# Two-layer hybrid network in fp32 on one core: half-partition operations get their own durations in the plan, the parameters arrive as 16 rows, and dummy products stand in gaps at both ends

## The chip, the cores and the metric

The program runs on one core of one Trainium2 chip. The core has a matrix engine (TensorE, PE in the profile; its weight loads are shown as PEld), a vector engine (VectorE, DVE), an activation engine (ScalarE, ACT), GpSimd (POOL) and a queue engine (SyncE, SP) that here issues every DMA. The metric is the device time of one execution in microseconds; lower is better. Results of TensorE land in PSUM, which this kernel uses as eight banks of 128 partitions by 512 fp32 values.

## The reference

A network of two layers on 1024 tokens by 1024 features in fp32, cut here to what is computed:

```python
for layer in range(2):
    h = rmsnorm(x, mix_norm[layer])
    y = sliding_window_attention(h, ...) if layer == 0 else hgrn2_recurrence(h, ...)
    x = x + y
    h = rmsnorm(x, mlp_norm[layer])
    x = x + square(relu(h @ w_up[layer])) @ w_down[layer]     # 1024 -> 4096 -> 1024
return rmsnorm(x, final_norm)
```

The attention has 16 query heads over 4 key/value heads of 64 features, a window of 128 tokens, partial rotary embedding and one sink logit per head. The recurrence is a gated linear recurrence over chunks of 64 tokens with 8 heads of 128 features.

## The kernel before

The activations lie transposed: features on the 128 partitions, 512 tokens (one half of the sequence) along the free axis. A matrix product in fp32 is made of three products of split operands (`mm3`): each factor is split into a high part in fp32r (`wh` for weights, made by a CAST on ACT or DVE) and the remainder (`wl`, made by a subtraction on DVE), and high x high, high x low and low x high are summed in one PSUM bank. Bank tags are `p` (four banks) and `q` (four banks). `wr` are raw weights as loaded (six buffers), `wh` and `wl` have five buffers each, `a` and `t` are tiles of 128x512, `m` a smaller pool of them, `sm` are tiny ones, `c` constants, `d` tiles in DRAM. The large products use one or two levels of Strassen's scheme.

No engine's order is written by hand. The program records all operations with their operands (`Schedule.add`), each with a planned duration for each engine that could do it. `forward` then lays them out in time with a list scheduler, engine by engine, by rank; `backward` works out the latest start (`late`) of each operation; four passes alternate and the best one is issued (`order`, `issue`). So a planned duration decides which engine does an operation and where it stands in that engine's row, and the engine then runs its row strictly in that order. `act`, `copy`, `tt` and `stt` (lines 435 to 461) give the durations: for ACT reading PSUM 52 ns and 0.834 ns per column, for DVE 70 ns and 1.04 ns per column, whatever the number of partitions.

The stages, with their places in the profiled execution:

- Head (0 to about 8 us). `first_loads` issues the loads of x, the parameters `par` (norm gains and bounds, 64 columns on 128 partitions) and the first weights. `warm` has TensorE multiply a zero tile by itself eight times (16 rows in the trace, since a product of plain fp32 runs as two). `scaled` multiplies x by a gain out of `par`, ACT for the high part and DVE for the low part.
- `qkv(0)` for the first half of the tokens (to about 82 us): three column groups of 512 columns. Group 0 holds keys and values, groups 1 and 2 queries. In each group four `p` banks (one per block of 128 tokens) collect 8 x 3 products each, 96 in all. When a group is complete, DVE reads the four banks with `stt` (scale by the token's factor, add the bias; `projected`, `keys_values`), and only then can the next group write those banks. `keys_values` also turns the keys by TensorE into a `q` bank and takes them out with half-partition operations on 64 partitions: `copy` on ACT for the high part and `tt` on DVE for the low part, 64x128 each, line 1202 onward.
- Attention of both halves, interleaved with `qkv(1)`, then the output projection (to about 330 us). `attend` (line 1206) takes turned queries out of a bank by one `act` and one `stt` on 64x512 each.
- MLP of layer 0 (to about 900 us), HGRN layer (to about 1450 us; `recurrence` copies score blocks of 64 partitions by 256 columns on ACT, lines 1505 to 1507), MLP of layer 1 (to about 2065 us).
- The end. `final` normalises the output, called three times: for the first half of the tokens (about 2038 us), and for the second half in two pieces of 256 tokens (about 2052 and 2065 us). `sum_squares` adds squares, once over seven of the eight feature tiles (`first`) and once over the eighth (`last`); `token_rstd` takes their means by TensorE products with a 128x1 constant into a `q` bank, and computes 1/sqrt in five tiny operations; `spread` turns the token factors into a 128-partition bank by products with the identity `self.ident` (tile `c67`). DVE multiplies three quarters of the output tiles by that bank, and POOL, which cannot read it, one quarter with a copy `rs` that ACT makes of the bank. Each result goes out by a DMA from SP.

Of the kernel before, what the change touches and what calls it, by code (L numbers as in the profile page):

```python
# [17 lines left out]
P = 128  # L18
# [13 lines left out]
HD = 64  # L32
# [115 lines left out]
class Schedule:  # L148
# [8 lines left out]
    def add(self, ways, outs, ins, tail=0.0, form=None, table=None):  # L157
# [4 lines left out]
        if any(isinstance(v, View) and v.buf.tag == "p" for v in ins):  # L162
            lead = max(lead, EVACUATE)
        op.rank, op.after, op.first = (len(self.ops) - lead, len(self.ops)), [], []
# [23 lines left out]
    def forward(self):  # L188
# [41 lines left out]
        while True:  # L230
# [131 lines left out]
class Net:  # L362
# [72 lines left out]
    def act(self, out, in_, func, n=TH, bias=None, scale=1.0, accum=None):  # L435
        kw, cost = {}, (52 if in_.buf.tag in "pq" else 94) + n * 0.834
# [11 lines left out]
    def copy(self, out, in_, n=TH, engines=("ACT",), psum=True):  # L448
        ways = {"ACT": self.call(self.nc.scalar.copy, out, in_) + ((52 if psum else 94) + n * 0.834,)}
# [3 lines left out]
    def tt(self, e, out, x, y, alu, n=TH):  # L453
        cost = {"DVE": 70 + n * 1.04, "Pool": 147 + n * 2.105}
# [4 lines left out]
    def stt(self, out, x, scalar, y, op0, op1, n=TH):  # L459
        self.op("DVE", self.nc.vector.scalar_tensor_tensor, [out], [x, scalar, y], 70 + n * 1.04 + 60 * isinstance(scalar, View),  # L460
# [71 lines left out]
    def token_rstd(self, acc, inner=1.0, outer=1.0, n=TH, keep=False, more=()):  # L532
# [50 lines left out]
    def square_relu(self, m, hf, c, psum):  # L583
# [6 lines left out]
        else:  # L590
# [7 lines left out]
            self.s.add({"ACT": (on_act, 2 * (94 + TH * 0.834)), "DVE": (on_dve, 70 + TH * 1.04)}, [c], [c])  # L598
# [534 lines left out]
    def first_loads(self):  # L1133
# [3 lines left out]
        self.x = [[None] * NH for _ in range(KT)]  # L1137
        for kt in range(KT):
# [5 lines left out]
            if kt == 0:  # L1144
                self.dma(self.par, self.io["par"], 4 * P * N_PAR)
# [31 lines left out]
    def keys_values(self, n, ps, r):  # L1177
# [16 lines left out]
        for i, (first, end) in enumerate(K_SPANS):  # L1194
# [540 lines left out]
```

## Time and profile before

| | us |
|---|---|
| median of 3 runs (lowest, highest) | 2078.83 (2077.93, 2079.97) |
| the profiled execution, its own time | 2078.63 |
| its span, from the first to the last instruction | 2076.9 |
| TensorE busy, share of the span | 2058.8, 99% |
| VectorE busy, share of the span | 1894.4, 91% |
| ScalarE busy, share of the span | 1109.9, 53% |
| mean granted TensorE clock | 0.997 |

Nearly all instructions carry line 416 (`issue` records them all there), so the groups are told apart by tiles and shapes. A busy TensorE says little by itself, since the ends of its matmuls are modelled; the views by window and by time show where its rows stop following one another, and how far apart they stand.

### The profile page before, as it was taken

To read this page: it belongs to the slowest core of one execution; us is meant where nothing else is said; L and a number is where in the kernel's file an instruction comes from. 1 tells how busy PE (TensorE), PEld (TensorE's weight loads), DVE (VectorE), ACT (ScalarE), POOL (GpSimd) and SP (SyncE) were. 2 spreads that over 40 slices of the span, in tenths; PEclk is the share of its full clock that TensorE was granted. 3 is DMA by queue.
4 is the path that set the end of the run, shared out by engine and by line. 5 is a ranking of instruction groups with operands and counts; after the bars stand their busy time and mean duration, and the time that the engine had idled before them with its cause. 6 is when DMAs were issued, how large, how long until landed. Compare 5 with 4: busy or idle time off the path is not lost.

```text
span 2076.9 us, 35708 instructions
## 1 busy us (share of the span) xinstructions
PE 2058.8 (99%) x12220; PEld 1746.1 (84%) x12220; DVE 1894.4 (91%) x3929; ACT 1109.9 (53%) x2265; POOL 58.2 (3%) x121
## 2 busy tenths in 40 slices
PE   9999999999999999999999999999999999999998
PEld 7778878888898888888888888888888888888887
DVE  8899999999999989989998888888999999998995
ACT  6465867655565423556444444443766556532453
POOL 4030000000000000000000000000000000000000
PEclk9999999999999999999999999999999999999999
DMA  6212368877779967641322222677887768996822
GB/s 214 81 56 72 118 218 262 290 223 247 226 246 306 339 218 246 220 137 67 109 95 99 103 102 90 214 237 235 284 265 248 238 224 265 309 315 212 270 64 82
DMA packets 225846, 407.43 MB, mean 196 GB/s; under 512 B 25344, under 2 KB 30464, under 8 KB 225664
## 3 DMA queue, kind: packets, MB, share of 16 engines
q1 hardware_dynamic: 225664, 405.16, 58.9%
q8 instruction: 96, 1.57, 0.3%
q14 instruction: 86, 0.70, 0.1%
HBM read 321.17 MB, written 83.89 MB: 195 GB/s over the span
## 4 chain that ended last, share of the span: by engine, by line
PE 96%; DVE 2%; issue 1%; ACT 1%; DMA 0%; POOL 0%; POOLq 0%; SPq 0%; ACTq 0%; DVEq 0%
PE p L416 51%; PE q L416 44%; DVE a L416 1%; DVE t L416 1%; ACT a L416 1%; DVE wl L416 0%; ACT t L416 0%; DMA wr<-in_wqkv 0%; DVE m L416 0%; ACT wh L416 0%; POOL a L416 0%; POOLq L1709 0%; SPq L416 0%; ACT m L416 0%; DVE sm L416 0%
## 5 line engine op out<-in xcount | busy, mean ns | idle before, releaser
L416 PE MATMUL p<-a,wh 128*128 128x512 f32 (+1 forms) x2880 | 806.3, 364 | 0.0
L416 PE MATMUL q<-a,wh 128*128 128x512 f32 x2112 | 653.2, 391 | 0.0
L416 PEld LDWEIGHTS p<-a,wh 128*128 128x128 f32 x2880 | 515.2, 189 | 83.1 <-issue 0.4
L416 PE MATMUL p<-a,wl 128*128 128x512 f32 (+1 forms) x1440 | 522.2, 363 | 0.0
L416 PEld LDWEIGHTS q<-a,wh 128*128 128x128 f32 x2112 | 389.7, 188 | 75.3
L416 PE MATMUL q<-a,wl 128*128 128x512 f32 x1056 | 410.6, 389 | 0.0
L416 PEld LDWEIGHTS p<-a,wl 128*128 128x128 f32 x1440 | 271.9, 189 | 40.0
L416 ACT CAST wh<-wr 128x512 fp32r<-128x512 f32 x252 | 155.8, 620 | 186.3 <-PE p L416 117.5
L416 DVE TENSOR_TENSOR wl<-wr,wh 128x512 fp32r<-128x512 f32 x352 | 240.6, 688 | 6.3 <-ACT wh L416 2.5
L416 DVE TENSOR_TENSOR wl<-m,wh 128x512 fp32r<-128x512 f32 x338 | 231.6, 686 | 11.1 <-ACT wh L416 5.8
L416 ACT CAST wh<-m 128x512 fp32r<-128x512 f32 x252 | 155.8, 620 | 154.1 <-PE q L416 88.7
L416 PEld LDWEIGHTS q<-a,wl 128*128 128x128 f32 x1056 | 198.4, 188 | 42.0
L416 ACT ACTIVATE t<-t 128x512 f32<-128x512 f32 x244 | 153.8, 632 | 113.6 <-DVE t L416 107.8
L416 DVE TENSOR_TENSOR a<-t,a 128x512 fp32r<-128x512 f32 (+2 forms) x314 | 207.3, 678 | 6.6 <-PE q L416 5.5
L416 DVE TENSOR_TENSOR t<-t,t 128x512 f32<-128x512 f32 (+3 forms) x337 | 196.8, 599 | 5.7 <-ACT t L416 4.5
L416 ACT COPY t<-q 128x512 f32<-128x512 f32 (+2 forms) x201 | 111.4, 559 | 97.8 <-PE q L416 84.7
L416 ACT CAST a<-t 128x512 fp32r<-128x512 f32 (+1 forms) x199 | 119.2, 611 | 66.3 <-PE q L416 40.3
L416 PE MATMUL p<-wh,a 128*128 128x512 f32 x384 | 127.6, 403 | 5.1 <-DVE a L416 4.1
L416 DVE TENSOR_TENSOR m<-wr,wr 128x512 f32<-128x512 f32 (+1 forms) x188 | 121.4, 646 | 3.3 <-DMA wr<-in_down 1.5
L416 DVE TENSOR_TENSOR t<-t,p 128x256 f32<-128x256 f32 x294 | 118.6, 414 | 0.0
L416 PEld LDWEIGHTS q<-t,t 128*64 128x64 f32 (+1 forms) x2160 | 95.9, 144 | 12.9 <-issue 8.1
L416 PE MATMUL q<-t,t 128*64 128x32 f32 (+2 forms) x2160 | 104.8, 229 | 0.2 <-ACT t L416 0.2
(129 smaller groups left out, 2387.0 us busy)
## 6 DMA issues: line engine op xcount, KB each, us to landing
t<-d SPq DMA_DIRECT2D x548, 256.0 KB, 4.1
d<-t SPq DMA_DIRECT2D x244, 256.0 KB, 3.3
wr<-in_down SPq DMA_DIRECT2D x224, 256.0 KB, 4.1
wr<-in_up SPq DMA_DIRECT2D x178, 256.0 KB, 3.9
wr<-in_win SPq DMA_DIRECT2D x68, 256.0 KB, 2.8
a<-d SPq DMA_DIRECT2D x60, 256.0 KB, 3.9
wr<-in_wqkv SPq DMA_DIRECT2D x48, 256.0 KB, 2.9
d<-a SPq DMA_DIRECT2D x48, 256.0 KB, 3.8
```

Of the source, the lines that this page charges most:

```text
L416: fn(*[place(a) for a in args], **{k: place(v) for k, v in kw.items()})
```

## The change

It has three parts that the planner then turns into a new order of the whole program.

1. Plan. Operations on half of the partitions get 125 ns more on ACT and 105 ns more on DVE (`HALF`): the 64x128 copies and subtractions in `keys_values`, the 64x512 ones in `attend`, the 64x256 copies in `recurrence`. The two-step square of a rectified tile on ACT gets 150 ns more. A new rule in `forward` lets an engine stay idle for a more urgent operation that becomes ready soon (`WAIT`). In `keys_values` DVE's subtraction is recorded before POOL's clearing.
2. Head. The parameters come as 16 rows of 512 values in one load, issued first; four TensorE transposes turn them into a `p` bank and ACT copies the bank to `par`. `warm` does ten products.
3. End, in `token_rstd` and `final`, wherever `more` is given, that is in all three calls of `final`: all means of `first` come before those of `last`; four dummy products of the identity with itself follow those of `first` and five more follow those of `last`, each set into a `q` bank of its own. For the two pieces of 256 tokens `spread` is done twice, into two banks, one for DVE and one for ACT's copy; and one pair of output tiles is multiplied and stored in two pieces.

The diff, cut to its core:

```diff
+HALF = {"ACT": 125.0, "DVE": 105.0}
+WAIT = 0.5
-WARM = 8
+WARM = 10
+ROWS = 16
...
+            if p and e != "PE" and op.late is not None:
+                soon = p[0][2]
+                gap, lost = p[0][0] - t, t + op.ways[e][1] - p[0][0]
+                if not soon.engine and soon.late is not None and gap < WAIT * lost and soon.late < t + op.ways[e][1] \
+                        and op.late > soon.late and len(soon.ways) >= 1:
+                    heapq.heappush(r, (op.rank, op))
+                    free_at[e] = p[0][0]
+                    continue
...
-    def warm(self, zero):
-        ps = self.psum()
-        for _ in range(WARM):
+    def warm(self, zero, n=WARM, tag="p"):
+        ps = self.psum(tag)
+        for _ in range(n):
             self.mm(ps[:, :P], zero, zero, True, True, P, 4)
...
-        for j in range(nb):
-            parts = [acc, *more]
-            for i, z in enumerate(parts):
-                self.mm(ps[:, j : j + 1], z[:, j * P : j * P + P], self.mean, i == 0, i == len(parts) - 1, P, 2)
+        parts = [acc, *more]
+        for i, z in enumerate(parts):
+            for j in range(nb):
+                first, last = (j == 0, j == nb - 1) if more else (True, True)
+                self.mm(ps[:, j : j + 1], z[:, j * P : j * P + P], self.mean, i == 0 and first, i == len(parts) - 1 and last, P, 2,
+                        skip_group_check=bool(more))
+            if more and z is acc:
+                self.warm(self.ident, 4, "q")
+        if more:
+            self.warm(self.ident, 5, "q")
...
+        rows = self.t()
+        self.dma(rows[:ROWS], self.io["par"], 4 * P * N_PAR)
+        ps = self.psum()
+        n = N_PAR // ROWS
+        for k in range(n):
+            self.op("PE", self.nc.tensor.transpose, [ps], [rows, self.ident], 109, ps[:, k * ROWS : k * ROWS + ROWS],
+                    rows[:ROWS, k * P : k * P + P], self.ident[:ROWS, :ROWS], form="whole")
+        self.copy(self.par, ps[:, :N_PAR], N_PAR)
...
-            if kt == 0:
-                self.dma(self.par, self.io["par"], 4 * P * N_PAR)
...
-                self.copy(dst, src, P)
+                self.copy(dst, src, P, more=HALF["ACT"])
+                self.tt("DVE", kl[g][r, c].only(n), src, dst.bitcast(F32), ALU.subtract, P, HALF["DVE"])
                 self.ts("Pool", ks[g][o, c].only(n), dst, 1.0, None, ALU.mult, None, P)
-                self.tt("DVE", kl[g][r, c].only(n), src, dst.bitcast(F32), ALU.subtract, P)
...
-                    self.act(s[r], pq[r], AF.Copy, scale=HD**-0.5)
-                    self.stt(s[o], pq[r], HD**-0.5, s[r].bitcast(F32), ALU.mult, ALU.subtract)
+                    self.act(s[r], pq[r], AF.Copy, scale=HD**-0.5, more=HALF["ACT"])
+                    self.stt(s[o], pq[r], HD**-0.5, s[r].bitcast(F32), ALU.mult, ALU.subtract, more=HALF["DVE"])
...
-        r, rs = self.spread(self.token_rstd(first, n=n, more=[last]), n), self.t()[:, :n]
-        self.copy(rs, r, n)
+        y = self.token_rstd(first, n=n, more=[last])
+        r, rs = self.spread(y, n), self.t()[:, :n]
+        self.copy(rs, self.spread(y, n) if n < TH else r, n)
...
+            step = 1 if n < TH and k == per else per
+            for i in range(0, per, step):
+                c = slice(i, i + step)
+                part = pair[:, c].only(*range(k + i, k + i + step))
+                self.tt(e, part, part, share.unsqueeze(1).to_broadcast([P, step, n]), ALU.mult, step * n)
```

What moves is seen in three places. In the rows below a tile's name has its buffer number and then its number in the program, which differ between the two programs for the same thing.

DVE in `qkv(0)`, just ahead of the read-out of column group 1 (`a<-p,sm,a`, banks p125 and on before, p127 and on after); `a<-a,c,a` are low parts of the second half's x, `t<-t,t` sums of squares, `t<-q,a` the 64x128 subtractions. Before:

```order
L416 TENSOR_TENSOR t120_196<-q124_668,a116_701 64x128
L416 SCALAR_TENSOR_TENSOR a224_843<-a210_545,c01_65,a223_609 128x512 [waits DMAHW2_49]
L416 TENSOR_TENSOR t229_665<-t229_665,t236_836 128x512 [waits Activation_49]
L416 TENSOR_TENSOR wl177_854<-wr175_662,wh176_845 128x512 [waits DMAHW0_49,Activation_49]
L416 SCALAR_TENSOR_TENSOR a226_858<-a211_555,c01_65,a225_722 128x512 [waits DMAHW3_49]
L416 SCALAR_TENSOR_TENSOR a228_865<-a212_571,c01_65,a227_729 128x512 [waits DMAHW4_49]
L416 TENSOR_TENSOR a91_872<-a90_548 128x256
L416 SCALAR_TENSOR_TENSOR a153_876<-p125_565,sm50_451,a61_396 128x512 [waits PE_49]
L416 SCALAR_TENSOR_TENSOR a156_881<-p126_579,sm50_451,a61_396 128x512 [waits PE_49]
```

After:

```order
L428 TENSOR_TENSOR wl179_831<-wr177_709,wh178_824 128x512 [waits DMAHW0_49,Activation_49]
L428 TENSOR_TENSOR t104_362<-q114_639,a100_379 64x128
L428 TENSOR_TENSOR t119_174<-q114_639,a115_727 64x128
L428 TENSOR_TENSOR t120_187<-q114_639,a116_733 64x128
L428 TENSOR_TENSOR t121_192<-q114_639,a117_737 64x128
L428 TENSOR_TENSOR t122_198<-q114_639,a118_743 64x128
L428 SCALAR_TENSOR_TENSOR a220_853<-a209_424,c01_65,a219_494 128x512
L428 SCALAR_TENSOR_TENSOR a155_861<-p127_578,sm52_473,a63_558 128x512 [waits DMAHW3_49,PE_49]
L428 SCALAR_TENSOR_TENSOR a158_867<-p128_590,sm52_473,a63_558 128x512 [waits PE_49]
```

Counted from the read-out of group 0 to that of group 1, DVE's row holds 66 instructions before and 59 after: four 64x128 subtractions, two `a<-a,c,a` and one 128x256 difference now stand behind the read-out.

ACT in the same column group; `wh<-wr` are the high parts of weights, `a<-q 64x128` the half-partition copies, `t<-a` squares. Before:

```order
L416 CAST a114_694<-q124_668 64x128
L416 CAST a115_697<-q124_668 64x128
L416 CAST a116_701<-q124_668 64x128
L416 ACTIVATE t231_714<-a207_497 128x512 [waits DVE_49]
L416 ACTIVATE a225_722<-a211_555,c01_65 128x512 [waits DMAHW3_49]
L416 ACTIVATE a227_729<-a212_571,c01_65 128x512 [waits DMAHW4_49]
L416 ACTIVATE t232_737<-a208_510 128x512 [waits DVE_49]
L416 CAST wh148_745<-wr147_466 128x512 [waits PE_49]
L416 CAST wh151_751<-wr150_480 128x512 [waits DMAHW5_49,PE_49]
```

After:

```order
L428 CAST a118_743<-q114_639 64x128
L428 CAST a115_727<-q126_647 64x128 [waits PE_49]
L428 CAST a116_733<-q126_647 64x128
L428 CAST wh172_754<-wr171_569 128x512 [waits DMAHW4_49,Activation_49]
L428 CAST wh153_760<-wr152_547 128x512 [waits DMAHW2_49,PE_49,Activation_49]
L428 CAST a117_737<-q126_647 64x128
L428 CAST wh147_772<-wr146_528 128x512 [waits DVE_49,DMAHW0_49,PE_49,Activation_49]
L428 CAST a118_743<-q126_647 64x128
L428 CAST wh150_785<-wr149_536 128x512 [waits DMAHW1_49]
```

The eight squares, which stood between and behind the copies, now stand in a row ahead of all of them (rows 43 to 50 of ACT's row, behind `a229`), each in a buffer of its own, where seven of the eight shared one before; the high parts that group 1 still needs (`wh147`, `wh150`, `wh153`) stand behind the copies. Over the attention layer, 24 CASTs that DVE did before are now ACT's.

PE at the end, where the first piece of 256 tokens of the second half is finished (`p5026` and `p5028` are its last bank, `q5883` and `q5887` the bank of means, `p5023` and `p5025` banks of the last piece). Before:

```order
L416 MATMUL p5026_21383<-a5848_24269,a5845_24223 128x256
L416 MATMUL p5026_21383<-a5847_24217,a5846_24275 128x256
L416 MATMUL q5883_24485<-c23_69,t5875_23906 128x1 [waits DVE_49]
L416 MATMUL p5023_21353<-a5812_24036,a5810_24025 128x256
L416 MATMUL p5023_21353<-a5813_24041,a5810_24025 128x256
L416 MATMUL p5023_21353<-a5812_24036,a5811_24033 128x256
```

After:

```order
L428 MATMUL p5028_21380<-a5849_24213,a5848_24298 128x256
L428 MATMUL q5887_24497<-c23_69,t5879_23773 128x1 [waits DVE_49,PE_49]
L428 MATMUL q5887_24497<-c23_69,t5879_23773 128x1
L428 MATMUL q5888_24502<-c67_67 128x128 [waits PE_49]
L428 MATMUL q5888_24502<-c67_67 128x128 x3
L428 MATMUL q5889_24508<-c67_67 128x128 [waits PE_49]
L428 MATMUL q5889_24508<-c67_67 128x128 x2
L428 MATMUL q5887_24497<-c23_69,t5886_24510 128x1 [waits Activation_49]
L428 MATMUL q5887_24497<-c23_69,t5886_24510 128x1
L428 MATMUL q5889_24508<-c67_67 128x128 x2
L428 MATMUL p5025_21354<-a5814_24046,a5812_24035 128x256
```

Seven of the nine dummy products (`c67` alone on the right) stand between the two sets of means and two behind them; before, products of the last piece stood there. In the call for the first half of the tokens the nine dummies stand likewise between products, four behind the first four means and five behind the others.

More of the change, by code (lines that the diff above doesn't have):

```diff
@@ L446, in act, with copy, tt @@
                 out, in_, func, scale=scale, table=TABLES.get(func), **kw)
[L448 to L449 removed]
+    def copy(self, out, in_, n=TH, engines=("ACT",), psum=True, more=0.0):
+        ways = {"ACT": self.call(self.nc.scalar.copy, out, in_) + ((52 if psum else 94) + n * 0.834 + more,)}
         ways["DVE"] = self.call(self.nc.vector.tensor_copy, out, in_) + (70 + n * (1.04 if psum else 0.52),)
         self.s.add({e: ways[e] for e in engines}, [out], [in_])
[L453 to L454 removed]
+    def tt(self, e, out, x, y, alu, n=TH, more=0.0):
+        cost = {"DVE": 70 + n * 1.04 + more, "Pool": 147 + n * 2.105}
         engines = ("DVE",) if e == "any" else (e,)
```

22 lines of the change are left out of this document (11 added, 11 removed).

## The prediction

> **What bounds the kernel now.** I read the page first, then the chain of waits, then windows chosen along it, then the rows by time at the four places where TensorE's rows do not follow one another.
>
> ```profile
> span 2076.9 us, 35708 instructions
> PE 2058.8 (99%) x12220; PEld 1746.1 (84%) x12220; DVE 1894.4 (91%) x3929; ACT 1109.9 (53%) x2265; POOL 58.2 (3%) x121
> PE 96%; DVE 2%; issue 1%; ACT 1%; DMA 0%; POOL 0%; POOLq 0%; SPq 0%; ACTq 0%; DVEq 0%
> ```
>
> TensorE is busy 2058.8 of 2076.9 us and carries 96% of the chain. Whatever a new order of the other engines can give is thus among some 18 us of idle time, the places where its clock is halved, and the few microseconds ahead of its first and behind its last product; every row added to TensorE costs its length wherever TensorE has no gap. The windows (busy us of PE, PEld, DVE, ACT and POOL with instructions, granted clock, DMA share, GB/s) say where the gaps are:
>
> ```profile
> core 0: us, PE busy (x) PEld busy (x) DVE busy (x) ACT busy (x) POOL busy (x), PEclk, DMA share, GB/s
> 54.00:58.05 4.05, 0.15 (x2) 0.03 (x1) 4.02 (x8) 0.62 (x1) 0.00 (x0) 1.00 0.21 65
> 55.06:58.47 3.41, 0.42 (x2) 0.41 (x3) 3.38 (x6) 0.00 (x0) 0.00 (x0) 1.00 0.25 77
> 58.47:61.89 3.42, 3.42 (x10) 2.64 (x9) 3.42 (x11) 0.00 (x0) 0.00 (x0) 0.50 0.09 23
> 62.00:300.00 238.00, 235.69 (x1361) 189.15 (x1360) 216.03 (x497) 157.18 (x497) 23.20 (x50) 1.00 0.32 104
> 300.00:2038.00 1738.00, 1737.79 (x10388) 1482.47 (x10387) 1604.56 (x3235) 906.03 (x1669) 8.58 (x20) 1.00 0.64 211
> 2038.00:2065.20 27.20, 27.20 (x232) 27.16 (x230) 16.39 (x40) 6.99 (x18) 2.59 (x2) 1.00 0.31 117
> 2065.51:2068.93 3.42, 0.83 (x6) 0.78 (x7) 1.50 (x7) 1.02 (x3) 0.00 (x0) 1.00 0.00 0
> ```
>
> One stall of 3.9 us at 54 us, with DVE busy throughout; 3.4 us at half clock right behind it, which cost 1.7 us more; 2.3 us of small waits over the rest of the attention layer; 0.2 us in 1738 us after that; none from 2038 to 2065 us, where `final` is called for the first time and the second. The reader is to see that the whole middle has nothing to win.
>
> The sums are made against the profiled execution, 2078.63 us, and the result is set against the median of the runs, 2078.83 us, 0.2 us more. A measurement of this kernel can tell about 0.2%, 4.2 us, from no change.
>
> **Column group 1 of the first projection.** DVE's and ACT's rows there, and twelve TensorE products in a row:
>
> ```profile
> 29.88 0.47 DVE L416 SCALAR_TENSOR_TENSOR t<-p,sm,a 128x256 f32<-128x256 f32 x1
> ...
> 33.39 0.18 DVE L416 TENSOR_TENSOR t<-t,t 128x32 f32<-128x32 f32 x1
> ...
> 52.28 1.19 DVE L416 TENSOR_TENSOR t<-q,a 64x128 fp32r<-64x128 f32 x4
> ...
> 55.38 1.40 DVE L416 SCALAR_TENSOR_TENSOR a<-a,c,a 128x512 fp32r<-128x512 f32 x2
> 56.70 0.41 DVE L416 TENSOR_TENSOR a<-a 128x256 f32<-128x256 f32 x1
> 57.15 2.73 DVE L416 SCALAR_TENSOR_TENSOR a<-p,sm,a 128x512 f32<-128x512 f32 x4
> ```
>
> ```profile
> 38.95 2.82 ACT L416 CAST a<-q 64x128 fp32r<-64x128 f32 x10
> 41.80 0.63 ACT L416 ACTIVATE t<-a 128x512 f32<-128x512 f32 x1
> 44.08 1.13 ACT L416 CAST wh<-wr 128x512 fp32r<-128x512 f32 x2
> ```
>
> ```profile
> 378.49 2.75 PE q L416 x12
> ```
>
> The four banks of group 1 are full at 54.0, but DVE reads them from 57.15: it had work left in its row. The plan counted a 64x128 subtraction as 70 + 128 x 1.04 = 203 ns and a 64x128 copy as 52 + 128 x 0.834 = 159 ns; the rows show 1.19 / 4 = 298 and 2.82 / 10 = 282 ns. So twenty of each made DVE 1.9 us and ACT 2.5 us later than planned. The added 105 and 125 ns give 308 and 284 ns: the new durations are the measured ones.
>
> What the new order makes of it, worked out in two ways. By difference: between the two read-outs DVE has 4 x 0.30 + 2 x 0.70 + 0.41 = 3.0 us less, so it reads from 57.15 - 3.0 = 54.1 instead; one read of 0.68 us and the way to TensorE leave a stall of 1.0 us. By ACT's row: the squares no longer wait for each other's buffer, so they run from about 33.5, when the rotary operations at 33.39 free their buffers, for 0.63 + 7 x 0.52 = 4.3 us, with casts' spacing of 1.13 - 0.62 = 0.51 as the nearest row; 18 copies at 0.282 take 5.1, two casts 1.1, one copy and `wh147` 0.9 us: ready at 44.9. TensorE wants it after 60 products at 2.75 / 12 = 0.229 and eight transposes at about 0.1, 14.5 us after group 1 began (54.0 - 23.0 = 31.0): 45.5. Its low part on DVE follows at about 45.9, 0.2 late. I take 0.8, between 0.2 and 1.0. A wait this short leaves the clock alone, as no window above with most of its time busy is followed by 0.50. The term is 0.8 - 3.9 - 1.7 = **-4.8**, at best -5.6, at worst -2.0, if 1.9 us of waiting halve the clock again.
>
> **The rest of the attention layer.** The same correction applies to 64x512 operations, and 24 casts pass from DVE (216 of 238 us busy) to ACT (157), which has the room: 24 x 0.51 = 12 us. At most the 2.3 us go; as a row rearranged by the same rules can also miss, the bound above is one more stall like that at 54 us, +4. I take **-1.0**, less than half of what is there.
>
> **HGRN layer and both MLPs.** 0.2 us is to be won. All of it is rearranged, 45 more casts pass to ACT (906 of 1738 us busy), and the 64x256 copies are planned longer: **0**, bounds -0.2 and +3, a stall of the known kind without its half clock.
>
> **The head.**
>
> ```profile
> 1.05 3.78 PE L416 MATMUL p<-t 128*128 128x128 f32 x16 [1.05 <-DVE t L416]
> ...
> 4.99 0.71 ACT L416 ACTIVATE a<-a,c 128x512 fp32r<-128x512 f32 x1
> ...
> 5.75 0.79 PE L416 MATMUL p<-wh,a 128*128 128x512 f32 x1 [0.92 <-DVE c L416]
> ...
> 6.34 0.63 PE L416 MATMUL p<-wl,a 128*128 128x512 f32 x1
> ...
> 6.77 0.63 PE L416 MATMUL p<-wh,a 128*128 128x512 f32 x1
> ...
> 8.48 1.22 PE L416 MATMUL p<-wh,a 128*128 128x512 f32 x2 [0.23 <-DVE a L416]
> ...
> 10.74 0.40 PE L416 MATMUL p<-wl,a 128*128 128x512 f32 x1
> ```
>
> Sixteen rows of warming take 3.4 us to the last one's start, at half clock; twenty take 4.2, so the four new transposes start at 5.5 and end about 5.9. The loads are not the reason: `par` is now issued first, and the first weight tile of that place arrived at 3.8. ACT's copy of 64 columns (0.25, as for other 64-column operations, and the way from TensorE) lets `a<-a,c` start at 6.45, and the first product at 6.45 + 0.71 + 0.05 = 7.2, against 5.75. The stall before 8.48 falls away, as DVE now does that low part at 7.4 to 8.1, ahead of the second weight tile. Products stand 0.43 apart until 10.7 and 0.23 after. By 10.7 there are 10.2 products before and 8.2 after: 2 x 0.23 = **+0.5**. If the clock comes up before 7.2, it is 15 by then: -1.2. If only at 14.0 (two windows of 3.41 on): +2.0.
>
> **Dummies and the double spread in the first two calls.**
>
> ```profile
> 2038.12 1.84 PE L416 MATMUL q<-c,t 128*128 128x1 f32 x16
> 2039.80 1.75 PEld L416 LDWEIGHTS p<-a,a 128*128 128x128 f32 x14
> 2039.82 1.92 PE L416 MATMUL p<-a,a 128*128 128x256 f32 x14
> ```
>
> Sixteen rows of the same weight load take 2039.82 - 2038.12 = 1.70 us, 0.106 each. Nine dummies are 18 rows, twice, and the second bank 4 rows: 40 x 0.106 = **+4.2**. Nothing hides them: TensorE is busy 27.20 of 27.20 us here, and nobody waits for a dummy. Bounds 3.8 (the second bank beside a wait) and 4.4.
>
> **The tail.**
>
> ```profile
> 2057.95 16.30 SPq L416 DMA_DIRECT2D out<-a x8
> ...
> 2065.15 0.28 PE L416 MATMUL q<-c,t 128*128 128x1 f32 x2
> ...
> 2066.74 0.83 PE L416 MATMUL q<-c,t 128*128 128x1 f32 x6 [1.31 <-ACT t L416]
> ...
> 2068.93 1.20 PE L416 MATMUL q<-c,sm 128*128 128x128 f32 x4 [1.36 <-DVE sm L416]
> ...
> 2070.16 1.88 DVE L416 TENSOR_TENSOR a<-a,q 128x512 f32<-128x512 f32 x3 [1.38 <-PE q L416]
> 2072.13 0.37 ACT L416 COPY t<-q 128x256 f32<-128x256 f32 x1 [4.13 <-DVE a L416]
> 2072.58 1.26 POOL L416 TENSOR_TENSOR a<-a,t 128x512 f32<-128x512 f32 x1 [12.92 <-ACT t L416]
> ```
>
> ACT's copy waits until DVE has done three products from the one bank, then POOL, then the last store, issued by 2057.95 + 16.30 = 2074.25. After: four mean rows and 14 dummy rows run from 2065.15 to 2067.06, past 2066.74, so the last four means end 0.1 later than now. The spread starts at 2069.0, at full clock: four rows 0.11 apart and a latency of 0.3, DVE from 2069.6 (now 2070.16). The second bank is 0.4 later, ACT's copy at 2070.0, POOL 2070.5 to 2071.8; DVE's four pieces end at 2071.6. SP issues the last two stores at 2071.8 and 2072.3, against 2073.9 for the last now: **-1.5**; -1.8 if the last store need not queue behind POOL's, -0.5 if the means come later than worked out.
>
> The clock here was halved at 2068.93: the window of 3.41 us before had 0.83 us of work, in two gaps of 1.3 and 1.4 us. The Trainium skill, "TensorE: Matmul & The Clock Gate", section "HAM oscillation — how this bites in real kernels", asks only that no idle gap exceed about 3.4 us; by that the four spread rows would not have run at half clock, the dummies would bring nothing and the tail would be -1.0. Four rows that took 1.20 us, against 0.106 for one with that weight load above, say otherwise, and the trace decides.
>
> **Sum.** 0.5 - 4.8 - 1.0 + 0 + 4.2 - 1.5 = -2.6 us; 2078.8 - 2.6 = **2076.2**.
>
> **Rivals.** First, the warm-up opens the clock. Twenty rows and four transposes keep TensorE busy from 1.05 to 5.9, 4.9 us, longer than a window of 3.41. The head is then -1.2, the sum -4.3: 2074.5, just faster. For it: a window that lies wholly inside is possible for (4.9 - 3.41) / 3.41 = 0.44 of the phases. Against it: 3.78 us of warming did not open it before, which had to wait until 10.7. The same page, section "Part 1: The HAM clock gate", has the clock released after about 3.4 us of sustained work seen through a free-running window, which fits. Second, every wait of the attention layer goes: -5.6 and -2.3 in place of -4.8 and -1.0, sum -4.7, 2074.1; for it, that the corrected durations agree with the rows, against it, that `wh147` comes on the minute. Third, on the other side: ACT becomes late. If `wh147` is 6 us late, at 51, TensorE waits 6 us and then has 1.7 at half clock; the term is +2.1 instead of -4.8, the sum +4.3, 2083.1, and from there it is slower; 8 us give 2085.1. For it: ACT has eight squares and eighteen copies ahead of that cast in one unbroken row, and 24 casts more than before elsewhere in the layer. Against it: each square has its own buffer, so nothing in that row waits for DVE's sums. Fourth, the change at the end does nothing: the clock falls all the same, the tail is -0.5, 2077.2, still no difference.
>
> **How the numbers follow.** The forecast, with the fourth, has 0.47. The first two, alone or together (2072.4 together), have 0.36; the third, at this place or another of the layer, has 0.17. All terms at their best give -7.3, 2071.5; the upper end takes in the third up to 7 us. So 2071.0 to 2084.0.
>
> **What would show it.** Right: no idle time at the second read-out, and no 0.50 window near 60 us; first product near 7.2; 36 rows of `q<-c` alone near 2038 and 2052 us with DVE idle beside them; ACT's last copy beside DVE's products instead of behind them, rows of the last spread 0.11 apart. Wrong: a TensorE wait for an ACT `wh` cast in the first 300 us longer than 2 us, or idle time in the HGRN layer above 1 us.

## The result and the profile after

The changed kernel takes 2074.11 us (median of 13 runs, 2072.69 to 2076.92) against 2078.37 before (13 runs, 2077.41 to 2079.97): a ratio of 0.9980, 95% interval 0.9971 to 0.9989. It is faster by 4.3 us, at the edge of what can be told from no change. The forecast was 2076.2 within 2071.0 to 2084.0. The profiled execution took 2074.11 us, its span 2072.3.

The page of the changed kernel, the lines that answer to those of before:

```profile
span 2072.3 us, 35730 instructions
PE 2062.5 (100%) x12290; PEld 1753.2 (85%) x12290; DVE 1908.8 (92%) x3870; ACT 1139.5 (55%) x2319; POOL 61.1 (3%) x121
PE 96%; issue 1%; DMA 1%; DVE 1%; ACT 0%; POOL 0%; POOLq 0%; SPq 0%; ACTq 0%
```

TensorE has 70 rows more and 3.7 us more of busy time, in a span 4.5 us shorter. DVE's 2% of the chain are 1% now, and DMA, which had none, has 1%. By window (columns as in the prediction), before and then after:

```profile
42.00:62.00 20.00, 16.10 (x65) 12.86 (x64) 19.13 (x41) 8.41 (x15) 9.85 (x19) 0.91 0.22 72
62.00:300.00 238.00, 235.69 (x1361) 189.15 (x1360) 216.03 (x497) 157.18 (x497) 23.20 (x50) 1.00 0.32 104
300.00:1000.00 700.00, 700.00 (x3698) 598.05 (x3697) 659.70 (x1293) 378.28 (x664) 0.98 (x4) 1.00 0.70 231
1450.00:2033.00 583.00, 583.00 (x2995) 500.22 (x2994) 549.83 (x1051) 317.11 (x552) 0.00 (x0) 1.00 0.73 242
```

```profile
42.00:62.00 20.00, 20.00 (x89) 16.31 (x88) 19.62 (x53) 7.57 (x16) 10.39 (x14) 1.00 0.39 120
62.00:300.00 238.00, 237.87 (x1384) 193.92 (x1383) 220.78 (x483) 171.35 (x523) 26.05 (x52) 1.00 0.34 111
300.00:1000.00 700.00, 698.99 (x3723) 596.07 (x3722) 661.01 (x1270) 387.78 (x684) 0.98 (x4) 1.00 0.70 228
1450.00:2033.00 583.00, 582.66 (x3005) 499.95 (x3003) 544.41 (x1023) 315.46 (x553) 0.00 (x0) 1.00 0.72 237
```

The stall at 54 us and its half clock are gone: 89 products in 20 us instead of 65. But from 300 to 1000 us TensorE now has 1.0 us without work where it had none.

Products are alike in both programs, so their starts can be compared at places up to which both have done the same work. The lag is the start after less the start before; a term is what the lag changed by over a stage:

```
place, by the time of before         lag     term                            measured   predicted
first product of qkv(0), 5.75        +1.52
last products of group 1, 52.9       +0.46   head                              +0.5       +0.5
in column group 2, 67.9              -5.32   end of column group 1             -5.8       -4.8
start of the MLP of layer 0, 303.6   -9.70   rest of the attention layer       -4.4       -1.0
ahead of the first final, 2029.5     -7.78   HGRN layer and both MLPs          +1.9        0
last p product, 2065.0               -3.33   dummies and bank in two calls     +4.45      +4.2
end of the span, 2076.9              -4.51   tail                              -1.2       -1.5
```

Two of these terms are sums. The +1.9 are +2.0 in the first MLP, -0.9 in the HGRN layer and +0.8 in the second MLP. The head's +0.5 was +0.2 at the end of column group 0 (30.8 us); the other 0.25 us came in small waits while group 1 ran.

Rows of the changed kernel at the head, at the second read-out and behind the last p product (starts, busy us, engine):

```profile
5.61 0.60 PE L428 MATMUL p<-c,t 16*128 16x16 f32 x4
...
7.27 0.80 PE L428 MATMUL p<-wh,a 128*128 128x512 f32 x1 [1.06 <-ACT a L428]
...
52.95 2.73 DVE L428 SCALAR_TENSOR_TENSOR a<-p,sm,a 128x512 f32<-128x512 f32 x4
...
2062.19 1.81 PE L428 MATMUL q<-c 128*128 128x128 f32 x14
...
2062.94 0.42 ACT L428 ACTIVATE t<-a 128x256 f32<-128x256 f32 x1 [2.06 <-DVE a L428]
...
2063.83 0.50 PE L428 MATMUL q<-c,t 128*128 128x1 f32 x4
...
2065.61 1.16 PE L428 MATMUL q<-c,sm 128*128 128x128 f32 x8 [0.72 <-DVE sm L428]
2066.36 1.95 DVE L428 TENSOR_TENSOR a<-a,q 128x256 f32<-128x256 f32 x4 [0.80 <-PE q L428]
2066.81 0.37 ACT L428 COPY t<-q 128x256 f32<-128x256 f32 x1 [2.04 <-PE q L428]
2067.25 1.26 POOL L428 TENSOR_TENSOR a<-a,t 128x512 f32<-128x512 f32 x1 [13.80 <-ACT t L428]
```

The spread's rows stand 0.11 us apart, and ACT copies its own bank 0.45 us behind DVE's first product; it used to come 1.97 us behind it. But the last means start at 2063.83, 2.13 us behind the last p product at 2061.70, where they came 1.71 behind it: ACT's square is done at 2063.36, and TensorE is still at its fourteen dummy rows.

### The profile page after: what moved, and what is told of

It reads as the page before. It is cut to its first block, busy times and chain, and to the rows that moved or that the text cites. A ratio compares the mean times of both kernels' runs of the same rounds, so it can differ in the third digit from the quotient of the medians.

```text
span 2072.3 us, 35730 instructions
## 1 busy us (share of the span) xinstructions
PE 2062.5 (100%) x12290; PEld 1753.2 (85%) x12290; DVE 1908.8 (92%) x3870; ACT 1139.5 (55%) x2319; POOL 61.1 (3%) x121
## 4 chain that ended last, share of the span: by engine, by line
PE 96%; issue 1%; DMA 1%; DVE 1%; ACT 0%; POOL 0%; POOLq 0%; SPq 0%; ACTq 0%
PE p L428 52%; PE q L428 44%; DMA d<-t 0%; ACT t L428 0%; DMA t<-d 0%; DVE t L428 0%; DMA wr<-in_up 0%; DVE m L428 0%; DVE wl L428 0%; DVE a L428 0%; POOL a L428 0%; ACT wh L428 0%; POOLq L1738 0%; ACT a L428 0%; SPq L428 0%
## 5 line engine op out<-in xcount | busy, mean ns | idle before, releaser
L428 ACT CAST wh<-wr 128x512 fp32r<-128x512 f32 x285 | 175.9, 621 | 182.1 <-PE p L428 138.5
L428 ACT CAST wh<-m 128x512 fp32r<-128x512 f32 x262 | 162.2, 621 | 152.0 <-PE q L428 78.8
L428 ACT ACTIVATE t<-t 128x512 f32<-128x512 f32 x228 | 143.7, 632 | 101.6 <-DVE t L428 97.5
```

The source lines that it names most:

```text
L428: fn(*[place(a) for a in args], **{k: place(v) for k, v in kw.items()})
```

## The experiments

The times before beside these runs were 2077.3 to 2078.3 us; ratios are against the kernel before on the same chip.

**The plan part alone, and the two ends alone.** The first kernel takes this from the change and nothing else:

```diff
+HALF = {"ACT": 125.0, "DVE": 105.0}
+WAIT = 0.5
-                self.copy(dst, src, P)
+                self.copy(dst, src, P, more=HALF["ACT"])
...
-            self.s.add({"ACT": (on_act, 2 * (94 + TH * 0.834)), "DVE": (on_dve, 70 + TH * 1.04)}, [c], [c])
+            self.s.add({"ACT": (on_act, 2 * (94 + TH * 0.834) + 150), "DVE": (on_dve, 70 + TH * 1.04)}, [c], [c])
```

> The kernel before with the plan part of the change alone (durations of half-partition operations, the longer square, the waiting rule, the recording order in keys and values); parameters, warming and end as before. Theory A, the plan part did all the good and the two ends cost time: by the trace of after the stall at 54 us and the half clock behind it are gone (-5.8 us), the rest of the attention layer is 4.4 us shorter, the MLPs and the HGRN layer together 1.9 us longer, -8.3 in all, so about 2070 us against 2078.4 before. Rival B, any new order of this program moves its waits about and the new head had as much to do with the lost stall as the durations: the stall at 54 us comes back in part, 2074 us or more.

Measured: 2069.32 us (2068.99 to 2070.20), ratio 0.9959 (0.9947 to 0.9972). The number is theory A's: the plan part is worth 8.5 us, and the two ends together cost 4.2 us as the two gains over the kernel before compare, or 4.8 as the two times do. Its terms are A's only in part. In its trace the end of column group 1 gives 5.8 us, but the rest of the attention layer gives 3.3 instead of 4.4, the HGRN layer and the MLPs lose 0.1 instead of 1.9, and the clock was released at 4.0 us, which put TensorE 0.6 us ahead at 52.9.

> The changed kernel with the plan part taken back (durations, waiting rule and recording order as before); the parameters as 16 rows, the ten warming products, the dummies and the second bank stay. Theory A: head +0.3 us, 36 dummy rows and 4 rows of a second bank in the first two calls of the end +4.45, tail -1.2, together +3.5: about 2082 us, and the stall of about 4 us near 54 us still stands, with a window of half clock behind it. Rival B: the stall at 54 us goes without the new durations too, 2075 to 2077 us.

The second is the changed kernel without these (and with the recording order and the square's duration of before):

```diff
-HALF = {"ACT": 125.0, "DVE": 105.0}
+HALF = {"ACT": 0.0, "DVE": 0.0}
...
-            if p and e != "PE" and op.late is not None:
+            if False:
```

Measured: 2085.58 us (2084.81 to 2087.12), ratio 1.0037 (1.0024 to 1.0049), slower than either theory said. Its lag to before shows why: the stall is there with 1.7 us without work instead of 3.9 and without the half clock, so B holds for a part of it. But two shorter ones of 0.95 and 0.43 us stand ahead of it, the first product comes 2.45 us late instead of 1.52, since DVE does a low part of x ahead of a weight cast, the clock, released at 5.35 us, is halved again from 8.76 to 12.17, and from 68 to 1545 us the lag goes from -0.46 to +3.61 in small waits. The two end terms come out as A has them: from the first call to the last p product it loses 4.46 us, and the tail gives 1.2. A new order throws the waits anew; the ends do not bring fewer of them.

**Durations or waiting rule.** The plan part was divided. The first kernel has all of it but the rule, that is without

```diff
-            if p and e != "PE" and op.late is not None:
-                soon = p[0][2]
...
-                    free_at[e] = p[0][0]
-                    continue
```

and the second has these lines alone.

> The kernel before with the new durations alone (half-partition operations, the longer square, the recording order in keys and values), without the waiting rule. Theory A, the durations took the stall at 54 us away, since they let the plan see how late DVE and ACT really are: the stall and the half clock behind it are gone (-5.8 us) and part of the 4.4 us in the rest of the attention layer too: 2069 to 2072 us. Rival B, the waiting rule did it (it is also what moves casts from DVE to ACT: with it ACT has 41 rows more than before, with the durations alone 34 fewer): the stall stands, 2076 to 2079 us. Rival C, any new order takes most of it away, as with the two ends alone, where 1.9 us of it were left: 2072 to 2076 us.

> The kernel before with the waiting rule alone, all durations as before. Theory A (durations): the stall at 54 us stands, 2076 to 2079 us. Rival B (waiting rule): it is gone, 2069 to 2072 us. Rival C (any new order): 2072 to 2076 us with 1 to 2 us of it left.

The durations alone: 2070.56 us (2069.78 to 2072.36), ratio 0.9966 (0.9954 to 0.9979). The rule alone: 2078.71 (2077.77 to 2082.87), 1.0007 (0.9998 to 1.0015), with this row of TensorE:

```profile
56.97 0.47 PE L426 MATMUL p<-wh,a 128*128 128x512 f32 x1 [3.45 <-DVE a L426]
```

Theory A: the durations took the stall away, and between group 1 and the MLP 3.7 us more. The rule moves casts to ACT (947 in its trace, 896 with the durations alone, 897 before), and does nothing to the time by itself.

**Which durations, and how exact.** Two kernels with one edit each to the plan part:

```diff
-                    self.act(s[r], pq[r], AF.Copy, scale=HD**-0.5, more=HALF["ACT"])
+                    self.act(s[r], pq[r], AF.Copy, scale=HD**-0.5, more=0.0)
```

(likewise the other operations beside those of `keys_values`), and

```diff
-HALF = {"ACT": 125.0, "DVE": 105.0}
+HALF = {"ACT": 250.0, "DVE": 210.0}
```

> The plan part of the change with the new durations for the 64x128 operations of keys and values alone (and the recording order there, and the waiting rule); the 64x512 operations of attend, the 64x256 copies of the recurrence and the square keep their old durations. Theory A, the stall at 54 us goes with the twenty 64x128 operations ahead of it, and the waits from 110 to 300 us with the 64x512 ones: lag at 62 us as with the whole plan part (-5.8 us over the group), but 2 to 4 us of waits back behind it: 2071 to 2073 us against 2069.3. Rival B, the 64x128 durations do it all: 2069 to 2070 us.

> The plan part with twice the added durations (250 and 210 ns instead of 125 and 105). Theory A, the gain comes from durations that agree with the rows of the trace, so durations that are too long by as much as the old ones were too short lose some of it: 2071 to 2075 us. Rival B, anything that makes the plan do these operations sooner has the same effect: 2069 to 2070 us.

With the 64x128 operations alone: 2072.34 us (2071.09 to 2077.24), ratio 0.9972 (0.9961 to 0.9983). Group 1 gains the same (the lag goes from 0.04 to -5.74), and most of the waits behind it are back: from there to the MLP it gains 0.8 us, where the whole plan part gains 3.3. That is theory A. The trace is of the slowest execution, 2077.24 us, which also lost 5.1 us around 705 us in the first MLP, by waits of up to 2.6 us and the half clock behind them:

```profile
705.85:709.26 3.41, 3.41 (x9) 2.67 (x8) 3.41 (x7) 1.83 (x4) 0.00 (x0) 0.50 1.00 342
```

The waits from 62 to 300 us lie ahead of that. The stretch from 62 to 300 us, first with the 64x128 durations alone, then with twice the added durations:

```profile
62.00:300.00 238.00, 236.09 (x1364) 190.11 (x1363) 220.07 (x486) 163.18 (x508) 22.95 (x50) 1.00 0.35 109
```

```profile
62.00:300.00 238.00, 238.00 (x1385) 194.50 (x1384) 219.54 (x482) 172.74 (x524) 21.20 (x49) 1.00 0.35 113
300.00:1000.00 700.00, 698.68 (x3724) 596.22 (x3723) 660.58 (x1271) 386.90 (x685) 0.97 (x4) 1.00 0.69 228
```

With the 64x128 durations alone TensorE gets 1364 products done here, about as many as before the change (1361); with twice the durations 1385, as many as after it (1384). Twice the durations give 2073.62 us (2070.43 to 2075.12), 0.9975 (0.9964 to 0.9986). That is A's number and not A's cause: in the attention layer durations too long do as well as the measured ones (B), 5.6 us behind group 1. What was lost is 1.9 us in the first MLP, 1.0 in the second and some in the head, in the profiled execution, which was the fastest; where the others lost 3 us more no trace shows. What the runs show is thus that the old durations were too short, not that the new ones must be exact. For the 64x256 copies of the HGRN layer only one in two agrees: where two stand in a row in the trace of before, the second starts 0.269 us behind the first and the next operation 0.378 behind the second, against 0.266 in the old plan and 0.391 in the new one.

**The dummies.** At issue they were left out of the changed kernel's own order, first in two calls, then in all:

```diff
-                op.ways[op.engine][0]()
+                if not getattr(op, "out", False):
+                    op.ways[op.engine][0]()
...
-                self.warm(self.ident, 4, "q")
+                self.warm(self.ident, 4, "q", self.calls < 3)
```

> The changed kernel in its own order, with the dummy products of the first two calls of the end left out (they compute nothing that is used); the nine of the last call stay. No other instruction changes its place. Theory A: the rows are pure cost, 36 x 0.112 = 4.0 us off 2074.1: 2070.1 us. Rival B: they stand in time in which TensorE would wait for the factors anyway: 2073 to 2074 us.

> The changed kernel in its own order, with all dummy products left out, those of the last call too. Theory A: the means of the last tile come 0.4 us sooner, since no dummies stand ahead of them, but the clock is halved before the last spread as it was before the change; its eight rows then stand 0.21 us apart instead of 0.11, so that the second bank, which POOL's product waits for, is full 0.9 us later: 0.5 us slower than with the last dummies alone, about 2070.6 us. Rival B, without the dummies the clock holds through gaps of 1.3 to 1.5 us (the Trainium skill, TensorE: Matmul & The Clock Gate, section HAM oscillation, asks for gaps under about 3.4 us; the trace of before showed the half clock behind two such gaps): 0.4 us faster than with the last dummies alone, about 2069.7 us, and the rows of the spread stand 0.11 us apart.

Both miss, and their executions lie too far apart to tell the two kernels from each other. Without the dummies of two calls: 2075.47 us (2071.67 to 2079.20), ratio 0.9986 (0.9977 to 0.9995); without any: 2074.85 (2072.97 to 2077.92), 0.9988 (0.9979 to 0.9996). The windows of the first of these kernels in its first two calls, and its rows in the first:

```profile
2031.90:2035.31 3.41, 2.82 (x24) 2.58 (x23) 0.83 (x5) 0.20 (x1) 0.00 (x0) 1.00 0.00 0
2035.31:2038.73 3.42, 3.42 (x17) 3.42 (x18) 1.61 (x3) 0.00 (x0) 0.00 (x0) 0.50 0.01 3
2048.97:2052.38 3.41, 2.26 (x18) 2.00 (x18) 1.49 (x7) 1.02 (x3) 0.00 (x0) 1.00 0.00 0
2052.38:2055.79 3.41, 3.41 (x18) 3.41 (x18) 1.95 (x4) 0.37 (x1) 1.28 (x1) 0.50 0.20 64
```

```profile
2032.01 1.84 PE L431 MATMUL q<-c,t 128*128 128x1 f32 x16
2033.71 0.84 PE L431 MATMUL p<-a,a 128*128 128x256 f32 x5
2035.14 1.94 PE L431 MATMUL q<-c,sm 128*128 128x128 f32 x8 [0.59 <-DVE sm L431]
```

Where the dummies stood TensorE now waits for the factors or the last square, 0.6 to 1.1 us at a time, and twice the clock is halved behind that: 1.7 us each. From the first call to the last p product this execution is 1.5 us longer with 4.0 us of rows less. So in this order the dummies cover a real wait. The new end made that wait itself: where the dummies are planned, only five `p<-a,a` products are left between the means and the spread.

At the very end A was right. The spread behind no dummies, in the second of these kernels, which had the means 0.4 us sooner:

```profile
2064.50 2.05 PE L430 MATMUL q<-c,sm 128*128 128x128 f32 x8 [1.37 <-DVE sm L430]
2065.73 1.95 DVE L430 TENSOR_TENSOR a<-a,q 128x256 f32<-128x256 f32 x4 [1.38 <-PE q L430]
```

Eight rows take 2.05 us instead of 1.16, and from the last p product to the end it is 11.30 us, against 10.64 with the dummies and 11.83 before. By the Trainium skill, "TensorE: Matmul & The Clock Gate", section "HAM oscillation — how this bites in real kernels", the rule is no idle gap above about 3.4 us, and by it the clock would have held (rival B). The longest gaps in these two kernels were 1.1 and 1.4 us, and the clock fell; the measurement decides.

**The first two calls as they were.** Last, the changed kernel with the end's three steps in the last call only, its five later dummies bound to follow the last means, so that up to the first call every engine keeps the changed order:

```diff
-        y = self.token_rstd(first, n=n, more=[last])
+        end = n < TH and tokens.stop == TH
+        y = self.token_rstd(first, n=n, more=[last], end=end)
...
-        self.copy(rs, self.spread(y, n) if n < TH else r, n)
+        self.copy(rs, self.spread(y, n) if end else r, n)
...
+                    self.mm(keep_up[:, :P], self.ident, self.ident, True, True, P, 4, late=[ps] if i else ())
```

> The changed kernel with the first two calls of the end as they were before the change: no dummies, each column's two means next to each other, one bank; the last call has the new end with its five later dummies behind the last means. Up to the first call of the end every engine's order is that of the changed kernel. Theory A, the 40 added rows are pure cost where TensorE has other work around the means, and the falls of the clock with the dummies left out came from the new order of the means, which leaves TensorE waiting with nothing but the dummies between: 2074.1 - 4.5 - 0.4 = 2069.2 us, no window of half clock before the last spread. Rival B, the falls come with the missing dummies whatever the order of the means: windows of half clock near 2035 or 2050 us, 2072 us or more.

Measured: 2069.14 us (2068.14 to 2073.12), ratio 0.9965 (0.9951 to 0.9978). Theory A, to 0.1 us in the time; over the kernel before beside it the gain is 8.2 us, 3.9 more than the changed kernel's. In the trace nothing is left of the 4.45 us between the first call and the last p product. The edit takes back the dummies and the order of the means together, so which of the two had moved the products away is not shown. The first call again has products where the dummies were, and no half clock:

```profile
2029.19 1.84 PE L428 MATMUL q<-c,t 128*128 128x1 f32 x16
2030.90 1.92 PE L428 MATMUL p<-a,a 128*128 128x256 f32 x14
2032.66 1.05 PE L428 MATMUL q<-c,sm 128*128 128x128 f32 x8
```

**The plan part with the new end, and with more warming.** The new end of the last experiment, put on the plan part alone; and on the plan part alone the last warming product issued three times more, with nothing else moved:

```diff
+MORE = 3
...
+            self.s.ops[-1].again = MORE if k == WARM - 1 else 0
...
-            op.ways[op.engine][0]()
+            for _ in range(1 + op.again):
+                op.ways[op.engine][0]()
```

> The plan part of the change, and the new end in the last of the three calls only: second bank, two pieces for one pair of output tiles, four dummy products behind the first means and five that must follow the last means, so that none delays these. The first two calls and the head are as before. Against the plan part alone (2069.3 us): theory A, the last product to the end took 11.83 us there and 10.64 in the changed kernel, of which 0.42 was dummies ahead of the last means; without these 10.2: -1.6 us, 2067.7 us. Rival B, the dummies that keep the clock need to be as many as they were, and the spread runs at half clock: 11.3, -0.5 us, 2068.8 us.

> The plan part of the change in its own order, with three more warming products (22 rows instead of 16), which end at 5.7 us, just ahead of the first product at 5.8; parameters as before. Theory A, the clock is released at the end of the first window of 3.41 us that is busy from end to end, and the windows lie differently in each execution: with work from 1.05 us on without a gap that is between 4 and 7.5 us in every execution, where a gap from 4.8 to 5.8 us put it off to 10.1 to 10.8 us in two of the profiles so far; products are 0.2 us longer each until then, so the time is 0 to 1.5 us shorter by the execution, -0.7 us in the median, about 2068.6 us. Rival B, the release has nothing to do with the length of the warming: 2069.3 us and a release after 10 us in most executions.

With the end: 2068.40 us (2067.21 to 2069.21), ratio 0.9954 (0.9942 to 0.9967), the lowest median of this study, though its executions overlap with those of the kernels next to it. It is 0.9 us under the plan part alone, between the theories, though from the last p product to the end it is 10.35 us, near A's 10.2. The plan part alone has 11.83 there in its trace, but the same rows took 11.31 in three other kernels' executions, in which the clock fell only behind the spread: the dummies can save the half clock only where it would have come.

With more warming: 2069.36 us (2069.07 to 2069.95), no gain. The clock is released at 6.1 us, as A says, and at 20 us TensorE is 2.5 us ahead of before. At 51 us it is 1.2 ahead: TensorE gets sooner to places where another engine sets the time, such as a wait of 0.6 us behind ACT's casts at 44 us. The trace of the plan part alone, where the clock happened to be released at 4.0, shows the same, 2.0 and 0.6.

**The waits in the MLPs.** In the changed kernel's chain of waits transfers stand ahead of all four places where TensorE then waits for ACT; the first three (start, length):

```profile
339.81 4.16 DMA d<-t
...
504.12 5.62 DMA t<-d
...
538.99 4.04 DMA wr<-in_up
```

The edit to the changed kernel:

```diff
-LOAD, STORE = 3000.0, 2000.0
+LOAD, STORE = 4000.0, 4000.0
```

> The whole change, with transfers planned at 4.0 us behind their issue instead of 3.0 (loads) and 2.0 (stores); the trace of after has landings of 4 to 6 us where TensorE waits for ACT in the MLP at 352, 510, 548 and 1604 us, 2.3 us of waits in all, and in its order with the dummies left out the same places took 4.9 us, since TensorE came there 2 us sooner. Theory A, these waits come from transfers that the plan thinks too short, and so do differences between executions: 2071.5 to 2072.5 us, and less than 1.5 us between the lowest and the highest. Rival B, they are an accident of this order and a new one has others: 2074 us or more, and as much between the executions as now (4.2 us).

Measured: 2074.21 us (2073.36 to 2075.23, 11 runs), ratio 0.9980 (0.9971 to 0.9989). The waits are gone, so is most of the spread between executions (1.9 us instead of 4.2), and the time is the same. Its windows:

```profile
300.00:1000.00 700.00, 699.86 (x3707) 596.91 (x3707) 662.89 (x1269) 388.85 (x688) 0.97 (x4) 1.00 0.69 228
1000.00:1450.00 450.00, 450.00 (x3674) 380.78 (x3671) 404.34 (x881) 221.99 (x468) 7.38 (x16) 1.00 0.44 147
1450.00:2033.00 583.00, 583.00 (x3003) 500.39 (x3002) 546.99 (x1028) 313.41 (x551) 0.00 (x0) 1.00 0.72 238
```

From 303 to 2029 us its lag to before goes from -6.68 to -6.70. What the waits gave back the new head took: in the order made with these values its first product starts at 8.49 us, 1.2 us later than in the changed kernel, and in the profiled execution the clock is released only at 13.9. So the forecast of the time failed by another stage, and transfers planned longer did take the waits away, as A says. That they were planned too short is not the whole cause: the plan part alone, with the transfers planned as before, lost 0.1 us over the same stages and had 1.2 us between its five executions. An order nearly without the waits is to be had with the old values too. The windows of the plan part alone:

```profile
300.00:1000.00 700.00, 699.75 (x3730) 597.20 (x3729) 661.51 (x1275) 386.90 (x683) 0.98 (x4) 1.00 0.69 229
1450.00:2033.00 583.00, 582.78 (x3013) 500.58 (x3012) 547.89 (x1044) 302.96 (x533) 0.00 (x0) 1.00 0.72 237
```

## Why the prediction was right or wrong

- The range held the time, and the sign was right. The forecast of -2.6 us counted as no difference by the 4.2 us that the prediction named; the measured -4.3 lies at that edge. The measured time is that of the second rival, 2074.1, every wait of the attention layer gone. That holds for its mechanism, as far as idle time shows it (0.1 us is left of 2.3 from 62 to 300 us), but that its sum came out is luck, by two errors of its own: the attention layer gained 10.2 us where the rival had 7.9, and HGRN layer and MLPs gave back 1.9.
- Column group 1, -4.8: right. The durations did it, as the experiment with them alone shows. Nothing was left of the 0.8 us of stall that the term kept: `wh147` came in time, and DVE read the banks at 52.95.
- Rest of the attention layer, -1.0: the step that failed is "at most the 2.3 us go". That bound was the idle time of a window. A product that starts late behind a small wait is shown busy up to its modelled end, so such waits are not idle time. Taken by the distance of each product's start to the next, against the usual distance for its size, the 1361 products of 62 to 300 us lost some 8 us where the distance was over 0.1 us longer than usual, changes between forms of product included; after the change the same stretch lost some 4. I also named the casts that pass to ACT as a ground; they pass through the waiting rule, which alone gains nothing. The 64x512 durations do most of it, as the run without them shows (0.8 us instead of 3.3); that run took back the 64x256 copies and the square too, but these stand in later stages.
- HGRN and MLPs, 0: mis-sized, +1.9, within its bounds of -0.2 and +3 as a sum. The bound of -0.2 failed by itself for the same reason as above: the HGRN layer gained 0.9 us, while the MLPs lost 2.8. I looked for late casts. Ahead of the waits in the MLPs stood transfers that landed 4 to 6 us after their issue.
- Head, +0.5: right in its mechanism, the first product at 7.27 where 7.2 was worked out; that the term came out at +0.5 is in part luck. In these two executions the clock was released at 10.14 instead of 10.68, which left +0.2, and small waits in group 1, which the term did not have, added 0.25. The first rival, the warm-up that opens the clock, happened in three of four traces with this head in this order (release at 4.4, 6.0 and 4.3 us; 10.1 in the one compared). It brings little: the lead of 2 us is lost again where ACT or the transfers set the time. In the changed kernel's order with the dummies of two calls left out, a lead of 2.1 us over the changed kernel at 475 us was 0.1 at 521.
- Dummies in the first two calls, +4.2: right against before, +4.45 (0.112 us a row instead of 0.106). "Nothing hides them" was right for the old order alone. The planner moved products away, so that taking only the dummies out gained nothing; undoing the new order of the means with them gained 5.0 (3.9 over the kernels before beside them).
- Tail, -1.5: near, -1.2. The last means came 0.42 us later, not 0.1, because fourteen rows at 0.112 do not fit into the wait for ACT's square. The fourth rival falls: the clock held, which was worth 0.7 us there. Where the clock of the old end fell later, its tail took 11.31 us instead of 11.83, so in such executions the new tail gains 0.7 and not 1.2.

## What to carry to other kernels

Where a planner sets the order, a duration of a small operation that is planned too short can show as a stall of another engine; first compare planned durations and transfer times with measured rows, then look at order. Bound what waits can give by start-to-start distances against the operation's own time, not by idle time in a window. Dummy work is worth its rows only where nothing useful can stand there: here in the last microseconds, not in the two calls that had products to put between.

## What was not expected of the hardware

- The busy time of TensorE as the profile shows it is not what the clock goes by. All half clock between the release and the end lasted 3.41 or 3.42 us, so I count in windows of that length. The window of 2031.90 to 2035.31 us above was busy for 2.82 of 3.41 us and half clock followed; 1.7 us of it were rows of one column, so that wider rows had about 1.0 us (0.3). The other window had 1.7 us of wider rows (0.5). A window with 0.64 of them (6.0 to 9.4 us in the kernel without dummies) kept the clock. That rows of one column count for little fits these three, but not a fourth: with the durations alone, 2055.56 to 2058.97 us was busy for 2.10 us, at most 1.7 of it wider rows (0.5), and the clock held. No run tested it by itself, and where the line lies is open.
- The release seems to ask for more than that: 16 rows of warming from 1.05 us released the clock at 3.98 in one execution, which makes 0.86 of the window before it, and not in another, where a window ended at 3.86 (counted back from the release at 10.68), 0.82. The windows lie differently in each execution, so two executions of one order can differ by 2 us at 20 us, as the changed kernel and the one without the dummies of two calls do.
